# A two-layer attention and state-space kernel: the contexts' chunk sums turned and summed as a tree, and the outputs' matrices loaded behind the last row turn

## The chip, the cores and the metric

One core of one Trainium2 chip runs the whole program. The metric is the device time of one execution in microseconds. TensorE, VectorE (DVE), ScalarE (ACT), GpSimd (POOL) and SyncE (SP, which here only issues DMAs) run side by side, each through its own instructions in order; semaphores join them. ScalarE's queue issues a few DMAs too.

## What is computed

512 latent tokens and 256 context tokens of width 1024, all in fp32, go through two layers. Layer 0 mixes tokens by attention, layer 1 by a state-space model in both directions; each is followed by a gated feed-forward block with a convolution over tokens. Contexts see only contexts. In layer 1 the contexts are needed for one thing: the state at their end, `h0`, from which the latents start.

```python
def s5_scan(u, lb_re, lb_im, bb_re, bb_im, h0, reverse):      # 64 groups of 16 channels, 64 states each
    bu_re = jnp.einsum('blgc,gnc->blgn', u, bb_re)
    bu_im = jnp.einsum('blgc,gnc->blgn', u, bb_im)
    ...                                                       # h0 enters at the first token
    _, _, h_re, h_im = lax.associative_scan(_complex_combine, (a_re, a_im, bu_re, bu_im), reverse=reverse, axis=1)

for d in range(2):                                            # forward and reverse
    hc_re, hc_im = s5_scan(u_c, ..., None, reverse)           # contexts
    h0 = (hc_re[:, fin], hc_im[:, fin])
    hl_re, hl_im = s5_scan(u_l, ..., h0, reverse)             # latents
    y_l = y_l + s5_readout(hl_re, hl_im, c_re[d], c_im[d])
```

## The kernel before

Tokens are gathered in chunks of eight, so that the recurrence inside a chunk is a matrix product: 256 contexts are 32 chunks (`NCC`), 512 latents 64 (`NCL`). The matrices `Pd` (inputs of a chunk to its sum of states) and `Qd` (inputs and incoming state to the outputs) are made early in the program, stored to HBM, and loaded again tile by tile: `Pt` is the name of a loaded tile of either, `ssm_ahead` (L1378) the generator that loads them ahead of use. 32 pairs of groups make 16 contexts' tiles of 512 KB in three buffers, two pairs in each.

The contexts' part, `ssm_contexts` (L1483), runs as jobs that are written out between the matrix products `dn` of layer 0's second feed-forward product (L145 to L147, three fp32r products for one fp32 product). It loads the tokens by chunks (`xcc`, L1493), copies them into another order on ScalarE (L1405), turns them on TensorE (`pu`, L1410), and multiplies them by the `Pt` tiles (`pi`, L1435: 64 output rows, the states, by 32 columns, the chunks). ScalarE copies each result to `Bc` (L1446). `half(0)` and `half(1)` then run the recurrence over the chunks on VectorE, each for half of the groups: `ssm_spans` (L1460 to L1464) goes through eight chunks one after the other, in four spans at once, 35 operations; `ssm_carry` (L1473 to L1476) then joins the four spans in three steps. The result is `C0` (`C` in the rows). The powers of the recurrence's factors come from the table `lam`, 1 MB.

The last four steps of the feed-forward block, each of 128 tokens, are finished by the post-norm: `po<-dn` (L727), the norm's factor (L157 to L161), the sum with the stream `px` (L732, loaded at L713, stored at L1017) and the next pre-norm (L1020, L1021). The normed latents go to HBM and are read back by chunks as `xc` (L1028), the last pair of loads on ScalarE's queue. `ssm` (L1528) then copies `xc` to `xq` (L1405), turns it (L1410), multiplies it by the latents' `Pt` tiles (L1435), runs spans and carries (L1460 to L1476), makes the states (L1592 to L1603) and the outputs (`py`, L1616 and L1621) with the `Qd` tiles, of which eight buffers of 384 KB exist.

The order on each engine is set by the framework's scheduler from its own time estimates; the order of issue on SP follows from it.

Of the kernel before, what the change touches and what calls it, by code (L numbers as in the profile page):

```python
# [9 lines left out]
FT = mybir.dt.float32  # L10
# [3 lines left out]
AF = mybir.ActivationFunctionType  # L14
OP = mybir.AluOpType
# [4 lines left out]
P = 128  # L20
# [13 lines left out]
G = 64  # L34
NS = 64
GC = 16
TC = 8
NCC = CTX // TC
# [12 lines left out]
def dap(ap, off, dims):  # L51
    return bass.AP(tensor=ap.tensor, offset=ap.offset + off, ap=[list(d) for d in dims])
# [79 lines left out]
class Kernel:  # L132
# [1242 lines left out]
            self.lay_powers(lam, part, pw[:, part])  # L1375
        return lam

    def ssm_ahead(self, loads, rooms):  # L1378


        tiles = []
        rooms = [(pool, tag, bufs) for pool, tag, bufs in rooms for _ in range(bufs)]
        for i in range(len(loads)):
            while len(tiles) < min(i + len(rooms), len(loads)):
                src, gp, n = loads[len(tiles)]
                pool, tag, bufs = rooms[len(tiles) % len(rooms)]
                shape = [P, n, *src.shape[2:]]
                k = math.prod(shape[1:])
                t = pool.tile([P, 1024 if tag == "raw" else k], FT, name="Pt", tag=tag, bufs=bufs)
                t = t[:, :k].rearrange("p (a b n) -> p a b n", a=n, n=P)  # L1390
                self.nc.sync.dma_start(t, src[:, gp:gp + n])
                tiles.append(t)
            if i == 0:
                yield
            yield tiles[i]
# [24 lines left out]
    def ssm_inputs(self, mats, Bs, us, nj, both):  # L1420
# [5 lines left out]
        for gp in range(0, G // 2, R):  # L1426
# [19 lines left out]
                    nc.scalar.activation(y, x, AF.Copy)  # L1446
            yield gp

    def ssm_spans(self, pool, B, blk):

        nc, v = self.nc, self.nc.vector
        nb, ns = B.shape[1], B.shape[2] // 8
        lr, li = (x[:, 0, blk:blk + nb].rearrange("p b r d g -> p b r (d g)") for x in self.lam)
        L = B.rearrange("p b (s k) r d g -> p b s k r (d g)", k=8)
        shape = [P, nb, ns, 2, 16]
        lr, li = (x[:, :, None].to_broadcast(shape) for x in (lr, li))
        for k in range(1, 8):
            t1 = pool.tile(shape, FT, name="t1", tag="t1", bufs=1)
            t2 = pool.tile(shape, FT, name="t2", tag="t2", bufs=1)
            v.tensor_tensor(t1, L[:, :, :, k - 1], lr, op=OP.mult)  # L1460
            for b in range(nb):
                v.tensor_tensor(t2[:, b], L[:, b, :, k - 1, ::-1], li[:, b], op=OP.mult)
            v.tensor_tensor(L[:, :, :, k], L[:, :, :, k], t1, op=OP.add)
            self.mark = v.tensor_tensor(L[:, :, :, k], L[:, :, :, k], t2, op=OP.add).ins  # L1464
            yield

    def ssm_carry(self, pool, i, o, x, add):

        v = self.nc.vector
        mr, mi = (y[:, 7, 2 * i:2 * i + 2].rearrange("p b r d g -> p b r (d g)") for y in self.lam)  # L1470
        x, add, o = (y.rearrange("p b r d g -> p b r (d g)") for y in (x, add, o))
        w = pool.tile([P, 2, 2, 2, 16], FT, name="cw", tag="cw", bufs=2)
        v.tensor_tensor(w[:, 0], x, mr, op=OP.mult)  # L1473
        v.tensor_tensor(w[:, 1], x[:, :, ::-1], mi, op=OP.mult)
        v.tensor_tensor(w[:, 0], w[:, 0], add, op=OP.add)
        self.mark = v.tensor_tensor(o, w[:, 0], w[:, 1], op=OP.add).ins  # L1476
# [6 lines left out]
    def ssm_contexts(self):  # L1483

        nc, v, su = self.nc, self.nc.vector, self.su
        self.banks = (("aux", 2),)
        self.lam_tile(su.tile([P, 2048], FT, name="lam"))
        self.C0 = su.tile([P, 2, 2, 2, 2, 8], FT, name="C0")
        x = self.sb[1].tile([P, 2, 2048], FT, name="xcc", tag="B", bufs=1)
        xcc = x[:, 0].rearrange("p (s c) -> p s c", s=TC)  # L1490
        xq = x[:, 1].rearrange("p (g s c) -> p g s c", g=16, s=TC)
        for a in range(4):
            nc.sync.dma_start(xcc[NCC * a:NCC * a + NCC],  # L1493
                              dap(self.xnd, a * (D // 4), [[TC * D, NCC], [D, TC], [1, D // 4]]))
        sc = self.pool("ssmc")
        si = self.pool("ssmi")
        uc = si.tile([P, 16, 4, NCC], FT, name="uc")
        mats = self.ssm_ahead([(self.Pd, gp, 2) for gp in range(0, G // 2, 2)], ((si, "Pt", 3),))
        next(mats)
        yield  # L1500
        for _ in self.ssm_turn(xcc, xq, uc, (nc.scalar,) * 4):
            yield
        Bc = [sc.tile([P, 2, NCC, 2, 2, 8], FT, name=f"Bc{i}") for i in range(2)]

        def half(i):
            yield from self.ssm_spans(sc, Bc[i], 2 * i)
            x = Bc[i][:, :, 7]
            for s_ in range(8, NCC, 8):
                last = s_ == NCC - 8
                o = self.C0[:, i] if last else sc.tile([P, 2, 2, 2, 8], FT, name="cc", tag="cc", bufs=3)  # L1510
                self.ssm_carry(su, i, o, x, Bc[i][:, :, s_ + 7])
                x = o
                yield

        first = half(0)
        for gp in self.ssm_inputs(mats, lambda b: Bc[b // 2][:, b % 2], lambda g: uc[:, g % 16, g // 16], NCC,
                                  lambda gp: False):
            if gp >= 12:
                next(first, None)
                next(first, None)  # L1520
            yield
        for _ in first:
            yield
        yield from half(1)
        si.release()
        sc.release()

    def ssm(self):  # L1528
        tc, nc, v = self.tc, self.nc, self.nc.vector
        ps, W, su = self.ps, self.W, self.su  # L1530
        lamR, lamI = self.lam
        up = self.pool("ssmv")
        u = up.tile([P, G, NCL], FT, name="u")
        uv = u.rearrange("p (a g) j -> p g a j", a=2)
        self.banks = (("aux", 2), ("aux", 2), ("big", 3))
        xq = self.sb[1].tile([P, 4, 8, TC, GC], FT, name="xq", tag="B", bufs=1)
# [4 lines left out]
        B = [x.tile([P, 2, NCL + 1, 2, 2, 8], FT, name="B", tag="B", bufs=1) for x in (self.sb[0], up)]  # L1541
        for i in range(2):
            nc.scalar.activation(B[i][:, :, 0], self.C0[:, i], AF.Copy)
        sp = self.pool("ssms")
        st = self.pool("ssmt")
        spans = [*(self.ssm_spans(st, B[0][:, b:b + 1, 1:], b) for b in range(2)), self.ssm_spans(st, B[1][:, :, 1:], 2)]
        for gp in self.ssm_inputs(self.mats, lambda b: B[b // 2][:, b % 2, 1:], lambda g: u[:, g], NCL,
                                  lambda gp: gp < 16):
            for b in range(min((gp + 2) // 8, 2)):
# [2 lines left out]
        self.sx.release()  # L1552
        W.behind, W.fence, W.limit = (self.mark,), None, self.glu0 + 4
        W.ensure(self.glu0 + 4)
        qs = self.ssm_ahead([(self.Qd, gp, 1) for gp in range(G // 2)],
                            ((sp, "Qt", 8),))
        with tc.issue_after(self.turned_in):
            next(qs)
        sq = self.pool("ssmq")
        NL = NCL // 8  # L1560

# [8 lines left out]
        def local(i):  # L1570

            for s_ in range(NL - 1):
                o = B[i][:, :, 8 * s_ + 8]
                self.ssm_carry(su, i, o, B[i][:, :, 8 * s_], o)

        zs = [sq.tile([P, NL, 8, 32], FT, name=f"z{i}") for i in range(2)]
        for z in zs:
# [50 lines left out]
        tiles = range(LAT // P)  # L1628
# [28 lines left out]

        first(0)
        local(0)
        for blk in range(4):  # L1660
            if blk == 2:
                with tc.issue_after(self.stated):
                    first(1)
                    local(1)
            turned(blk, outputs(blk, states(blk)))
# [161 lines left out]
```

## Time and profile before

| what | value |
|---|---|
| time, median of 3 runs | 1690.97 us (1689.34 to 1693.05) |
| profiled execution | 1691.25 us, span 1689.5 us |
| TensorE, busy share of the span | 92% |
| VectorE | 63% |
| ScalarE | 41% |
| GpSimd | 4% |
| DMA, mean rate | 156 GB/s |

The time is that of a whole execution; the span runs from the first to the last record of the profile, and is 1.75 us shorter. Busy shares are means over stages that differ: an engine with 63% may be the one that everything waits for in one stretch.

### The profile page before, as it was taken

How to read it: one execution, taken by the hardware profiler on the slowest of the kernel's cores; microseconds unless marked ns; L12 is line 12 of the kernel's file. 1: busy time of each engine (PE TensorE's matmuls, PEld its weight loads, DVE VectorE, ACT ScalarE, POOL GpSimd, SP SyncE). 2: the span in 40 equal slices, each digit the busy share in tenths (PEclk: the TensorE clock that was granted, in tenths of full speed). 3: DMA queues.
4: the chain of work that ended last, by engine and by line, in shares of the span. 5: the costliest groups of instructions: out<-in, count | busy, mean ns of one | idle time of the engine just before them, and what ended most of it. 6: DMA issues, size and time to landing. Idle time of an engine off the chain costs nothing.

```text
span 1689.5 us, 25153 instructions
## 1 busy us (share of the span) xinstructions
PE 1548.3 (92%) x9652; PEld 1245.0 (74%) x9652; DVE 1071.1 (63%) x2225; ACT 695.2 (41%) x1370; POOL 67.0 (4%) x86
## 2 busy tenths in 40 slices
PE   5999689999999999989999999227999999999997
PEld 2776459888888887767788887226778887788886
DVE  4564587769777778767654847699346655455334
ACT  4465457746433433233343442331145443333322
POOL 0111140000000000000000000000011000000000
PEclk7999799999999999999999999568999999999999
DMA  9424460077345667695774685654443234433421
GB/s 301 148 71 128 166 216 26 26 247 248 132 139 174 186 172 208 134 236 143 207 257 136 195 266 200 203 197 127 151 133 117 88 112 125 127 98 114 148 75 50
DMA packets 222173, 262.96 MB, mean 156 GB/s; under 512 B 20974, under 2 KB 172438, under 8 KB 221414
## 3 DMA queue, kind: packets, MB, share of 16 engines
q1 hardware_dynamic: 221334, 260.76, 50.3%
q8 instruction: 76, 1.25, 0.3%
q10 hardware_dynamic: 336, 0.54, 0.1%
q14 instruction: 43, 0.35, 0.1%
q0 software_dynamic: 384, 0.07, 0.0%
HBM read 223.37 MB, written 35.85 MB: 153 GB/s over the span
## 4 chain that ended last, share of the span: by engine, by line
PE 80%; DVE 10%; DMA 4%; ACT 2%; SPq 2%; issue 1%; ACTq 0%; POOL 0%; DVEq 0%
PE up L145 12%; PE up L147 11%; PE up L146 11%; PE dn L145 6%; PE dn L146 6%; PE dn L147 6%; PE acc L145 2%; PE acc L147 2%; PE acc L146 2%; PE glu L147 2%; PE glu L145 2%; PE glu L146 2%; PE macc L287 2%; PE py L1621 1%; DMA wm<-in_w_mod 1%; PE wo L145 1%
## 5 line engine op out<-in xcount | busy, mean ns | idle before, releaser
L109 DVE TENSOR_TENSOR whl<-wraw,whl 128x1024 fp32r<-128x1024 f32 x206 | 250.8, 1222 | 175.5 <-ACT whl L108 173.9
L108 ACT ACTIVATE whl<-wraw 128x1024 fp32r<-128x1024 f32 x206 | 216.6, 1055 | 207.4 <-PE dn L147 100.1
L145 PE MATMUL up<-b,whl 128*128 128x256 f32 (+1 forms) x728 | 244.8, 340 | 5.8 <-ACT whl L108 4.8
L147 PE MATMUL up<-b,whl 128*128 128x256 f32 (+1 forms) x728 | 242.7, 335 | 0.0
L146 PE MATMUL up<-b,whl 128*128 128x256 f32 (+1 forms) x728 | 242.3, 335 | 0.2 <-DVE b L339 0.2
L146 PE MATMUL dn<-whl,hs 128*128 128x512 f32 x440 | 171.7, 392 | 0.0
L147 PE MATMUL dn<-whl,hs 128*128 128x512 f32 x440 | 170.9, 392 | 0.0
L145 PE MATMUL dn<-whl,hs 128*128 128x512 f32 x440 | 170.7, 392 | 0.0
L145 PEld LDWEIGHTS up<-b,whl 128*128 128x128 f32 x728 | 137.0, 189 | 32.1 <-issue 9.9
L147 PEld LDWEIGHTS up<-b,whl 128*128 128x128 f32 x728 | 137.1, 189 | 17.7 <-issue 3.4
L146 PEld LDWEIGHTS up<-b,whl 128*128 128x128 f32 x728 | 137.7, 189 | 15.9 <-issue 1.8
L862 DVE SCALAR_TENSOR_TENSOR ga<-up,cw,ga 128x511 f32<-128x511 f32 (+1 forms) x132 | 86.9, 659 | 93.3 <-ACT ga L858 91.8
L146 PE MATMUL up<-c,whl 128*128 128x512 f32 (+1 forms) x384 | 142.6, 373 | 0.1
L147 PE MATMUL up<-c,whl 128*128 128x512 f32 (+1 forms) x384 | 141.9, 372 | 0.0
L145 PE MATMUL up<-c,whl 128*128 128x512 f32 (+1 forms) x384 | 140.8, 375 | 1.0 <-DVE c L338 1.0
L858 ACT ACTIVATE ga<-up,cw 128x512 f32<-128x512 f32 x66 | 46.5, 705 | 159.9 <-PE up L147 158.3
L862 DVE SCALAR_TENSOR_TENSOR h<-up,cw,h 128x511 f32<-128x511 f32 (+1 forms) x132 | 86.8, 658 | 35.4 <-ACT h L858 34.2
L145 PEld LDWEIGHTS dn<-whl,hs 128*128 128x128 f32 x440 | 82.7, 188 | 18.4 <-ACT ga L858 0.4
L147 PEld LDWEIGHTS dn<-whl,hs 128*128 128x128 f32 x440 | 82.7, 188 | 18.0
L146 PEld LDWEIGHTS dn<-whl,hs 128*128 128x128 f32 x440 | 82.7, 188 | 17.8
L145 PEld LDWEIGHTS up<-c,whl 128*128 128x128 f32 x384 | 71.3, 188 | 18.0 <-issue 4.5
L147 PEld LDWEIGHTS up<-c,whl 128*128 128x128 f32 x384 | 72.3, 188 | 13.4 <-issue 0.4
(345 smaller groups left out, 2840.4 us busy)
## 6 DMA issues: line engine op xcount, KB each, us to landing
wraw<-in_w_up SPq DMA_DIRECT2D x88, 512.0 KB
wraw<-in_w_mod SPq DMA_DIRECT2D x80, 512.0 KB
wraw<-in_w_down SPq DMA_DIRECT2D x66, 512.0 KB
Pt<-Pd SPq DMA_DIRECT2D x32, 512.0 KB
wraw<-in_w_o SPq DMA_DIRECT2D x24, 512.0 KB
Pt<-Qd SPq DMA_DIRECT2D x32, 384.0 KB
wm<-in_w_mod SPq DMA_DIRECT2D x16, 512.0 KB
Pd<-Pb SPq DMA_DIRECT2D x16, 512.0 KB
```

The costliest lines, as they stand in the source:

```text
L108: nc.scalar.activation(w[:, 0], r, AF.Copy)
L109: e.tensor_tensor(w[:, 1], r, w[:, 0], op=OP.subtract)
L145: nc.tensor.matmul(out, a[0], b[0], start=start, stop=False)
L146: nc.tensor.matmul(out, a[0], b[1], start=False, stop=False)
L147: nc.tensor.matmul(out, a[1], b[0], start=False, stop=stop)
L287: nc.tensor.matmul(acc[32 * q:32 * q + 32], self.cT[:, k, :], w[:, 256 * q:256 * q + 256], start=(k == 0), stop=(k == KD - 1))
L858: nc.scalar.activation(o, acc, AF.Identity, scale=c[:, 1:2], bias=c[:, 3:4])
L862: nc.vector.scalar_tensor_tensor(x, acc[:, a + s:b + s], c[:, tap:tap + 1], x, op0=OP.mult, op1=OP.add)
L1621: nc.tensor.matmul(y[hs, i], x, t[hs, 2 + 2 * ri + d], start=False, stop=ri + d == 2)
```

## The change

Four edits, all in layer 1's state-space part.

1. The contexts' inputs come out by chunks. `ssm_inputs_turned` multiplies with the tokens as the stationary operand (32 columns, the chunks) and the matrix as the moving one (256 columns: two directions, real and imaginary, 64 states): 64 products of 32x256, four groups of them on the four quarters of a bank. A copy on ScalarE (`pe`, one buffer) and four turns on TensorE (`pb`) bring each result back to states by chunks, and the same copies to `Bc` follow. One group of products goes ahead of the turns of the group before.
2. The contexts' recurrence is a tree. `ssm_sums` joins neighbours, then pairs, then fours, in three levels of five operations, with powers 1, 2 and 4; `ssm_carry` takes the table as an argument.
3. The contexts use a small table `lamc` of the powers 1, 2, 4 and 8 (four loads); the full table `lam` is loaded in `ssm`.
4. The loads of the first `Qd` tiles are created ahead of the latents' inputs, and the first of those tiles is written first by a 1x1 copy on ScalarE from the last element of `xq`, so that its load comes behind the turn of `xq`.

```diff
+    def ssm_inputs_turned(self, mats, Bs, us, nj, pool):
...
+        def turn(e, gp):
+            b = self.bank([P, 2, 2, R, nj], "pb")
+            for d in range(2):
+                for ri in range(2):
+                    nc.tensor.transpose(b[:, d, ri].rearrange("p a j -> p (a j)"),
+                                        e[:, d, ri].rearrange("p a n -> p (a n)"), self.ident)
...
+            b = self.bank([P, 2, 2, 2, NS], "pi")
+            for par in range(2):
+                for i in range(R):
+                    nc.tensor.matmul(b[nj * i:nj * i + nj, par].rearrange("p d r n -> p (d r n)"), us(32 * par + gp + i),
+                                     pairs[i][:, 2 * par:2 * par + 2].rearrange("p d x -> p (d x)"),
+                                     start=True, stop=True)
+            pairs = pairs[R:]
+            e = pool.tile([P, 2, 2, 2, NS], FT, name="pe", tag="pe", bufs=1)
+            nc.scalar.activation(e.rearrange("p d r a n -> p a d r n"), b, AF.Copy)
+            if waiting:
+                turn(*waiting)
+                yield waiting[1]
+            waiting = e, gp
...
+    def ssm_sums(self, pool, B, blk, lam):
...
+        for i in range(3):
+            h, n = 1 << i, B.shape[2] >> i + 1
+            lr, li = (x[:, i, blk:blk + 2].rearrange("p b r d g -> p b r (d g)") for x in lam)
+            E, O = (B[:, :, j - 1::2 * h].rearrange("p b m r d g -> p b m r (d g)") for j in (h, 2 * h))
+            for j in range(2):
+                t = pool.tile([P, 2, B.shape[2] // 2, 2, 16], FT, name="t", tag="t", bufs=1)[:, :, :n]
+                if j:
+                    for b in range(2):
+                        v.tensor_tensor(t[:, b], E[:, b, :, ::-1], li[:, b, None].to_broadcast([P, n, 2, 16]), op=OP.mult)
+                else:
+                    v.tensor_tensor(t, E, lr[:, :, None].to_broadcast([P, 2, n, 2, 16]), op=OP.mult)
+                v.tensor_tensor(O, O, t, op=OP.add)
+                yield
...
-        self.lam_tile(su.tile([P, 2048], FT, name="lam"))
+        lam = su.tile([P, 2, 4, 4, 2, 2, 8], FT, name="lamc")
+        for i in range(4):
+            nc.sync.dma_start(lam[:, :, i].rearrange("p a b r d g -> p a (b r d g)"),
+                              dap(self.lamd, ((1 << i) - 1) * P, [[2048, P], [1024, 2], [1, P]]))
...
-            yield from self.ssm_spans(sc, Bc[i], 2 * i)
+            yield from self.ssm_sums(sc, Bc[i], 2 * i, lam)
...
+                if behind is not None and not tiles:
+                    self.nc.scalar.activation(t[0:1, 0:1], behind, AF.Copy)
...
+        qs = self.ssm_ahead([(self.Qd, gp, 1) for gp in range(G // 2)],
+                            ((sp, "Qt", 8),), xq[0:1, 3, 7, 7, 15:16])
+        next(qs)
```

The order of instructions shows where the scheduler puts the pieces. On TensorE, at the end of the feed-forward block, this stood before: the last `dn` (tokens' steps of whl_10261) are followed at once by the latents' turns, the contexts' last product being 51 `dn` further up.

```order
L146 MATMUL dn<-whl_10261,hs 128x512
L147 MATMUL dn<-whl_10261,hs 128x512
L1410 MATMUL pu<-ident,xq 128x128 x20
L1435 MATMUL pi<-u,Pt 64x64 x7
```

And this stands there now (whl_10072 is the last weight tile):

```order
L1462 MATMUL pb<-ident,pe 128x128 x4
L145 MATMUL dn<-whl_10072,hs 128x512
L146 MATMUL dn<-whl_10072,hs 128x512
L147 MATMUL dn<-whl_10072,hs 128x512 x2
L145 MATMUL dn<-whl_10072,hs 128x512
L1476 MATMUL pi<-Pt,uc 32x256 x6
L146 MATMUL dn<-whl_10072,hs 128x512
L147 MATMUL dn<-whl_10072,hs 128x512
L1476 MATMUL pi<-Pt,uc 32x256 x2
L1462 MATMUL pb<-ident,pe 128x128 x4
L1476 MATMUL pi<-Pt,uc 32x256 x6
L1462 MATMUL pb<-ident,pe 128x128 x4
L1412 MATMUL pu<-ident,xq 128x128 x24
```

The last eight products of the contexts and the last two groups of turns have moved behind the last `dn`. Further up, the products stand in pieces of 10, 6 and 2 with a group of four turns between; before they stood in five blocks of 48 and a rest of 16.

On VectorE, ahead of the post-norm's first `po<-dn` of the last two steps, the rows of half 1 now are (Bc_9514 is its tile; the carries that follow are three times the last four rows):

```order
L1503 TENSOR_TENSOR t<-Bc_9514,lamc 128x1024
L1504 TENSOR_TENSOR Bc_9514<-Bc_9514,t 128x32x32
L1501 TENSOR_TENSOR t<-Bc_9514,lamc 128x512 x2
L1504 TENSOR_TENSOR Bc_9514<-Bc_9514,t 128x32x32
L1503 TENSOR_TENSOR t<-Bc_9514,lamc 128x2x256
L1504 TENSOR_TENSOR Bc_9514<-Bc_9514,t 128x16x32
...
L1533 TENSOR_TENSOR cw<-cw,Bc_9514 128x64
L1534 TENSOR_TENSOR C_9265<-cw 128x64
L727 TENSOR_TENSOR po<-dn,rows_9253 128x512 x2
```

Before, 35 operations of `ssm_spans` stood in the same place, ahead of the same `po<-dn`; nothing else has moved past it.

On SP, behind the last `xc` loads of its queue, this is the order now, with the last waits of each row (the fourth step's pair of loads, then the outputs' and the latents' matrices):

```order
L1028 DMA xc<-po 16x8x512 [waits DMAHW1_49,DVE_49]
L1028 DMA xc<-po 16x8x512 [waits DMAHW2_49]
L1393 DMA Pt<-Qd 128x768 [waits DMAHW5_49]
L1393 DMA Pt<-Qd 128x768 [waits DMAHW6_49]
L1393 DMA Pt<-Qd 128x768 [waits DMAHW7_49,Activation_49]
L1393 DMA Pt<-Qd 128x768 [waits DMAHW0_49,DVE_49]
L1393 DMA Pt<-Qd 128x768 [waits DMAHW1_49]
```

Before, the eight `Qd` loads stood in the same place; the third of them now has a wait for ScalarE, the 1x1 copy behind the copies to `xq`, and the others stand behind it on this queue.

## Rows read from the trace of the kernel before

**Rows 1.** The table of stretches: length, busy time and instructions by engine, clock, DMA
```profile
1041.00:1056.00 15.00, 11.28 (x50) 9.01 (x48) 14.05 (x48) 1.68 (x5) 0.00 (x0) 0.99 0.05 20
1056.00:1085.00 29.00, 0.00 (x0) 0.00 (x0) 20.00 (x66) 6.88 (x16) 0.00 (x0) 0.50 0.66 205
1062.50:1063.00 0.50, 0.00 (x0) 0.00 (x0) 0.50 (x1) 0.50 (x2) 0.00 (x0) 0.50 0.53 213
1064.00:1064.50 0.50, 0.00 (x0) 0.00 (x0) 0.50 (x1) 0.00 (x0) 0.00 (x0) 0.50 0.04 8
```

**Rows 2.** TensorE's timeline, 989 to 1087 us: start, length, engine, line, operation, count, idle before
```profile
989.78 1.04 PE L1410 MATMUL pu<-ident,xcc 128*128 128x128 f32 x8
990.58 0.48 PE L145 MATMUL dn<-whl,hs 128*128 128x512 f32 x1
...
1000.43 0.39 PE L145 MATMUL dn<-whl,hs 128*128 128x512 f32 x1
1000.75 2.99 PE L1435 MATMUL pi<-uc,Pt 128*64 128x32 f32 x96
...
1004.00 0.39 PE L147 MATMUL dn<-whl,hs 128*128 128x512 f32 x1
...
1038.92 1.13 PE L1435 MATMUL pi<-uc,Pt 128*64 128x32 f32 x32
...
1051.44 0.39 PE L145 MATMUL dn<-whl,hs 128*128 128x512 f32 x1
...
1051.89 0.39 PE L147 MATMUL dn<-whl,hs 128*128 128x512 f32 x1
1086.03 4.30 PE L1410 MATMUL pu<-ident,xq 128*128 128x128 f32 x20 [33.74 <-ACT xq L1405]
```

**Rows 3.** VectorE's timeline, 1041 to 1056 us, same columns
```profile
1041.24 0.43 DVE L1460 TENSOR_TENSOR t<-Bc,lam 128x256 f32<-128x256 f32 x1 [3.10 <-ACT Bc L1446]
...
1053.18 0.23 DVE L1473 TENSOR_TENSOR cw<-Bc,lam 128x64 f32<-128x64 f32 x1
...
1055.43 0.68 DVE L727 TENSOR_TENSOR po<-dn,rows 128x512 f32<-128x512 f32 x1
```

**Rows 4.** ScalarE's timeline, 988 to 1088 us, same columns
```profile
988.24 2.19 ACT L1405 ACTIVATE xcc<-xcc 128x512 f32<-128x512 f32 x4 [3.18 <-DMA Pt<-Pd]
...
1040.09 1.12 ACT L1446 ACTIVATE Bc<-pi 128x256 f32<-128x256 f32 x2 [5.42 <-PE pi L1435]
...
1077.31 1.29 ACTq L1028 DMA_DIRECT2D xc<-po  x2
1085.34 2.19 ACT L1405 ACTIVATE xq<-xc 128x512 f32<-128x512 f32 x4 [12.07 <-DMA xc<-po]
```

**Rows 5.** TensorE's timeline at two places where the modulation stands in other work
```profile
562.88 1.07 PE L287 MATMUL macc<-wraw,cT 128*32 128x256 f32 x16
...
1383.91 0.39 PE L147 MATMUL up<-c,whl 128*128 128x512 f32 x1
1384.23 0.62 PE L287 MATMUL macc<-wraw,cT 128*32 128x256 f32 x4
...
1385.12 0.40 PE L146 MATMUL up<-c,whl 128*128 128x512 f32 x1
```

**Rows 6.** The DMA issues on SP's timeline, 1061 to 1084 us
```profile
1061.93 4.20 SPq L1017 DMA_DIRECT2D xd<-px  x2
...
1074.53 8.92 SPq L1391 DMA_DIRECT2D Pt<-Qd  x8
```

**Rows 7.** ScalarE's groups by shape, 0 to 500 us: busy, mean ns
```profile
L1213 ACT ACTIVATE tst<-ptab,sg 128x512 f32<-128x512 f32 x6 | 7.1, 1188 | 0.5 <-PE ptab L1212 0.4
```

**Rows 8.** VectorE's groups by shape, 1017 to 1060 and 1120 to 1200 us
```profile
L1462 DVE TENSOR_TENSOR t<-Bc,lam 128x128 f32<-128x128 f32 x27 | 6.7, 285 | 0.0
...
L1603 DVE TENSOR_TENSOR S<-B,z 128x1024 f32<-128x1024 f32 x4 | 4.9, 1216 | 0.0
...
L1464 DVE TENSOR_TENSOR B<-B,t 128x512 f32<-128x512 f32 x7 | 4.8, 691 | 0.2
```

More of the change, by code (lines that the diff above doesn't have):

```diff
@@ L1376, in lam_powers, with ssm_ahead @@
         return lam
-    def ssm_ahead(self, loads, rooms):
+    def ssm_ahead(self, loads, rooms, behind=None):
         tiles = []
@@ L1447, in ssm_inputs @@
             yield gp
+    def ssm_inputs_turned(self, mats, Bs, us, nj, pool):
+        nc = self.nc
+        R = P // nj
+        pairs, waiting = [], None
+        def turn(e, gp):
[4 more added lines that the diff above has]
+                                        e[:, d, ri].rearrange("p a n -> p (a n)"), self.ident)
+            o = Bs(gp // 8)
+            for d in range(2):
+                x = b[:, d, :, :, ::-1] if d else b[:, d]
+                nc.scalar.activation(o[:, :, :, d, gp % 8:gp % 8 + R].rearrange("p j r g -> p r g j"), x, AF.Copy)
+        for gp in range(0, G // 2, R):
+            while len(pairs) < R:
+                t = next(mats)
+                pairs += [t[:, i] for i in range(t.shape[1])]
+            b = self.bank([P, 2, 2, 2, NS], "pi")
[11 more added lines that the diff above has]
+            waiting = e, gp
+        turn(*waiting)
+        yield waiting[1]
@@ new lines, in ssm_sums @@
+    def ssm_sums(self, pool, B, blk, lam):
+        v = self.nc.vector
+        for i in range(3):
[11 more added lines that the diff above has]
+                yield
@@ L1465, in ssm_spans, with ssm_carry @@
             yield
-    def ssm_carry(self, pool, i, o, x, add):
+    def ssm_carry(self, pool, i, o, x, add, lam):
         v = self.nc.vector
-        mr, mi = (y[:, 7, 2 * i:2 * i + 2].rearrange("p b r d g -> p b r (d g)") for y in self.lam)
+        mr, mi = (y[:, y.shape[1] - 1, 2 * i:2 * i + 2].rearrange("p b r d g -> p b r (d g)") for y in lam)
         x, add, o = (y.rearrange("p b r d g -> p b r (d g)") for y in (x, add, o))
@@ L1486, in ssm_contexts @@
         self.banks = (("aux", 2),)
-        self.lam_tile(su.tile([P, 2048], FT, name="lam"))
+        lam = su.tile([P, 2, 4, 4, 2, 2, 8], FT, name="lamc")
+        for i in range(4):
+            nc.sync.dma_start(lam[:, :, i].rearrange("p a b r d g -> p a (b r d g)"),
+                              dap(self.lamd, ((1 << i) - 1) * P, [[2048, P], [1024, 2], [1, P]]))
+        lam = [lam[:, j] for j in range(2)]
         self.C0 = su.tile([P, 2, 2, 2, 2, 8], FT, name="C0")
@@ L1510, in half @@
                 o = self.C0[:, i] if last else sc.tile([P, 2, 2, 2, 8], FT, name="cc", tag="cc", bufs=3)
-                self.ssm_carry(su, i, o, x, Bc[i][:, :, s_ + 7])
+                self.ssm_carry(su, i, o, x, Bc[i][:, :, s_ + 7], lam)
                 x = o
@@ L1515, in ssm_contexts @@
         first = half(0)
-        for gp in self.ssm_inputs(mats, lambda b: Bc[b // 2][:, b % 2], lambda g: uc[:, g % 16, g // 16], NCC,
-                                  lambda gp: False):
+        for gp in self.ssm_inputs_turned(mats, lambda b: Bc[b // 2][:, b % 2], lambda g: uc[:, g % 16, g // 16], NCC, si):
             if gp >= 12:
@@ L1530, in ssm @@
         ps, W, su = self.ps, self.W, self.su
+        up = self.pool("ssmv")
+        self.lam_tile(up.tile([P, 2048], FT, name="lam"))
         lamR, lamI = self.lam
-        up = self.pool("ssmv")
         u = up.tile([P, G, NCL], FT, name="u")
@@ L1554, in ssm @@
         W.ensure(self.glu0 + 4)
[L1555 to L1558, printed above, removed]
         sq = self.pool("ssmq")
@@ L1573, in local @@
                 o = B[i][:, :, 8 * s_ + 8]
-                self.ssm_carry(su, i, o, B[i][:, :, 8 * s_], o)
+                self.ssm_carry(su, i, o, B[i][:, :, 8 * s_], o, self.lam)
         zs = [sq.tile([P, NL, 8, 32], FT, name=f"z{i}") for i in range(2)]
```

## The prediction, made before the changed kernel was run

> **What bounds the kernel now.** I read the page first: TensorE is by far the busiest engine, so the time moves much only where it stands still or where its stream gets longer or shorter. Then the table of stretches, which shows the one long hole of this layer [rows 1]: between 1056 and 1085 us TensorE does nothing, VectorE is busy for 20.00 of 29 us. Then TensorE's and VectorE's timelines on both sides of the hole. TensorE ends the first feed-forward block with the `dn` of 1051.89, and starts again with the turn `pu` of 1086.03, after 33.74 us idle [rows 2]. In front of the hole VectorE runs half 1 of the contexts' sums from 1041.24 on, carries from 1053.18, and only then the first post-norm step `po<-dn` at 1055.43 [rows 3]. From there a chain of VectorE and ScalarE leads to the last two `xc` loads, issued on ScalarE's queue at 1077.31, and ScalarE starts on them at 1085.34 [rows 4]. So the time of this place is made of four parts: when the last `dn` ends, plus how far half 1 sticks out behind it, plus 22 us of a chain that is not touched, plus the load of `xc`. In the kernel before, half 1 sticks out by only 55.43 − 52.12 = 3.3 us (the last `dn` is taken to end one spacing, 0.23, after its start), since nearly all of it lies beside the last 51 `dn`.
>
> **A: TensorE up to the last dn.** Removed there: 256 contexts' matmuls of 32 columns, in five blocks and a rest. One block takes 1004.00 − 1000.43 − 2 × 0.225 = 3.12 us out of the stream (the spacing of `dn` without a break is (1051.89 − 1051.44)/2 = 0.225); the rest, busy 1.13 where a block is 2.99, takes 3.12 − 1.86 = 1.26 [rows 2]. Sum 16.9 us. Added ahead of the last `dn`: by the order of the instructions one piece of 10 matmuls, six pieces of 6, five of 2, and six of four transposes. The trace has no matmul with 32 stationary columns and 256 moving ones here, but the modulation's `macc` is one in all but name [rows 5]: two instructions (four records) take 1385.12 − 1383.91 − 0.45 = 0.76 out of the stream, eight (sixteen records) are busy 1.07 against 0.62, so a second round of four costs 0.45 more. A piece of 2 is one round (0.76), a piece of 6 is two because its third and fourth column groups come twice (1.21), the piece of 10 three (1.66). Four transposes: half of the eight at 989.78, which take (990.58 − 989.78) + 0.10, so 0.45. Together 1.66 + 6 × 1.21 + 5 × 0.76 + 6 × 0.45 = 15.4. **A = −1.5 us.** Bounds: with no loss at a change of form, 14.5 rounds × 0.45 + six turns of 0.23 make 7.9, so −9; with 0.3 us of waiting at each of a dozen pieces, +2.
>
> Each `macc` piece costs about 0.3 us over its 0.45 of matmul, that is, the change of form is dear and the kernel now does twelve instead of six of them here [rows 5]. The Trainium skill, TensorEngine Tiling (Array Packing), Tiling Modes, says that a change of tiling mode drains TensorE, which speaks against cutting the inputs into small pieces between the `dn`. The same page, Overview, promises up to 4× for 32 columns; by that alone the 64 matmuls would cost 16 rounds and A would be near −9. By the rows it is −1.5.
>
> **B: TensorE at the contexts' turn.** In the order the eight first turns of `xcc` now stand 8 `dn` earlier. Before they start at 989.78, 1.5 us after ScalarE began the copies of `xcc` (988.24, after 3.18 of waiting for a DMA) [rows 2, 4]: they are on time and no more. Eight `dn` earlier is 1.8 us, which TensorE will wait. The power table ahead of `xcc` on SP's queue is 512 KB in 512-byte rows in place of 1 MB in long rows, with four issues for one. I take the landing as unchanged: **B = +1.8** (0 if the smaller table lets `xcc` land that much earlier, 3.2 if the extra issues delay it).
>
> **C: half 1 behind the last dn.** This is the large term. By the order, the last two `dn` are now followed by the rest of the inputs: two matmuls of the last group, the turn of group 6, six matmuls of the last group, its turn. Call the end of the last `dn` E. The copy `pe` of group 6 ends near E + 0.5, its turn near E + 1.3. The last six matmuls need the 16th `Pt` tile. There are three such buffers, so its load is issued only when group 6 has read tile 13, about 0.5 us ahead of E. The nearest transfer of that size with the engines free is the 512 KB store issued at 1061.93: moving by 1062.5, done by 1064.0 [rows 1, 6], 2.1 us; with what it takes to tell TensorE I take E + 3.0 (2 to 3.5). Then six matmuls to E + 4.0, the `pe` copy of 512 elements to E + 4.7 (between half of the pair of 1.12, 0.56 for 256 elements, and 1.19 for a strided copy of 512 [rows 4, 7]), turn E + 5.3, two `Bc` copies E + 6.5 (1.12 a pair).
>
> VectorE then does the whole of half 1, since its first sum reads the tile that the last copy writes. Three levels of five operations: three of 1024 and two of 512 elements, then three of 512 and two of 256, then three of 256 and two of 128. With 1.22, 0.69, 0.43 and 0.285 [rows 3, 8]: 5.04 + 2.93 + 1.86 = 9.8, and the carries, which are the same, 1055.43 − 1053.18 = 2.25. So 12.1 us, to E + 18.6. Only 2.1 less than the 14.2 of before (1041.24 to 1055.43), though operations fall from 35 to 15. `po<-dn` waits behind all of it on VectorE. Against 3.3 before: **C = +15.3** (14 to 18). The DMA engines, 5% busy from 1041 to 1056, and ScalarE cover none of it.
>
> What is queued behind: the post-norm chain with its stores, the `px` loads, which wait for half 1 in both kernels, and both pairs of `xc`. All of it shifts as one; nothing in the 22 us from `po<-dn` to the last `xc` issue depends on the removed operations.
>
> **D: the last xc load and the outputs' matrices.** Before, eight `Qd` loads of 384 KB go out on SP's queue from 1074.53 on over 8.92 us, and the last `xc` pair, issued at 1077.31, has not reached ScalarE before 1085.34, 8.0 us [rows 4, 6]. By the order, after the change two `Qd` go out there and the third waits for a 1x1 copy on ScalarE behind the `xq` copies, with five more behind it: 2.3 of 3.1 MB are out of the way. A pair that meets nothing would need about the 2.1 us of the store plus its own issue of 0.65: 2.8. With 0.8 MB and the other pair still ahead I take 4.0, so −4.0. Late next are those six `Qd` tiles, which go in front of nine `Pd` loads of the latents; seven tiles are already there, so this costs at most part of a tile, and the small copy 0.3: +0.8. **D = −3.2** (−4.7 to +0.5). The full table, loaded later, goes behind `Pd` loads far ahead of its use: nothing; if its cover is gone, 1 MB is about 3 us.
>
> **Sum:** −1.5 + 1.8 + 15.3 − 3.2 = **+12.4 us**, on the profiled 1691.25, which is 0.28 above the median of the runs: **1703.4 us** as a median.
>
> **Rivals.**
> - *The load of xc gains nothing.* Two Qd tiles and the other pair may be enough to hold it, or the six tiles then hold back the latents' `Pd`. Then D is 0 to +1: 1707. For it: the load took 8 us also because both pairs read short rows. Against it: 2.3 MB less in front. Chance 0.15. This is also the case that part of the change does not do what it says.
> - *TensorE waits inside the stream.* One `pe` buffer and two banks mean that each piece waits for ScalarE's copy of the group before, and the `Pt` tiles come in threes to groups of two. In the row order the next two matmuls stand only 4 to 12 `dn` behind, 0.9 to 2.7 us, for a copy of 0.6 to 1.2 plus ScalarE's other work. At 0.7 us for six groups A is +2.7: 1707.6. For it: no slack at the last groups. Against it: before shows no waiting for `Pt` there. Chance 0.15.
> - *The matmuls overlap fully and the dn end early.* A at −9: 1696. Against it are the `macc` rows. Chance 0.12.
> - *Not slower.* As the last, but a round costs half of `macc`'s, and so less than 5 us for all pieces: then `dn` ends 12 us earlier and the sum is within 1 us of zero, 1691 to 1692. It decides from the point where the pieces ahead of the last `dn` take under 6 us in place of 15.4; none of the rows has a round below 0.45. Chance 0.06, nearly all of it "no change".
> - *The forecast*, 1703.4, from 1699 to 1706: 0.52.
>
> **How the numbers follow.** A measurement of this kernel tells 0.2% (3.4 us) from no change. The range leaves out "not slower" and the worst pile-up of the two rivals above: 1696 to 1709. Slower by over 0.2% are all cases but "not slower" and a few mishaps: 0.90; same 0.06; faster 0.04.
>
> **What would show it.** Right: in the changed profile, about 19 us between the last `dn` and `po<-dn`, with VectorE idle for some 6 of them and the tree without a break after; some 45 us from the last `dn` to the turn `pu<-xq`, where it was 34.1; the last matmuls waiting for a `Pt` DMA; `xc` on ScalarE 4 us after its issue. Wrong for A: pieces of 2 well under 0.7 or waits named at them. Wrong for C: half 1's first operation within 4 us of the last `dn`, or operations of 1024 elements far from 1.22. Wrong for D: 7 us or more from issue to the copy. The forecast fails as a whole if VectorE runs `po<-dn` ahead of the tree, which the order excludes.

## The result: 0.7% slower, and the profile after

The changed kernel takes 1702.63 us (median of 4; 1701.72 to 1705.71), the kernel before, run beside it, 1691.20: ratio 1.0071, 95% interval 1.0053 to 1.0088, 11.4 us. The prediction said 1703.4. The profiled execution takes 1701.9 us, 10.65 more than that of before.

The two traces are laid side by side at the last `dn`. It starts at 1049.92, where it was 1051.89 [rows 2]. Those 2 us are not of the change: the `dn` that stands 205 places ahead of the last, before the contexts' first turn, is already 1.95 us earlier (984.66 against 986.61). In the profiles of e1 to e4 below, which do not differ there, it stands between 984.2 and 988.8.

TensorE's timeline of the changed kernel from the contexts' first turns, and around the last `dn` (start, length, engine, line, operation, count, idle before):

```profile
987.13 1.18 PE L1412 MATMUL pu<-ident,xcc 128*128 128x128 f32 x8 [0.95 <-ACT xcc L1407]
...
1048.59 1.06 PE L1476 MATMUL pi<-Pt,uc 128*32 128x256 f32 x12
...
1049.92 0.39 PE L147 MATMUL dn<-whl,hs 128*128 128x512 f32 x1
1050.24 0.63 PE L1476 MATMUL pi<-Pt,uc 128*32 128x256 f32 x4
1050.80 0.66 PE L1462 MATMUL pb<-ident,pe 128*128 128x128 f32 x4
1052.89 1.06 PE L1476 MATMUL pi<-Pt,uc 128*32 128x256 f32 x12 [1.44 <-DMA Pt<-Pd]
1054.71 0.66 PE L1462 MATMUL pb<-ident,pe 128*128 128x128 f32 x4 [0.76 <-ACT pe L1481]
```

The last group's matmuls stand behind the last `dn` and wait for their `Pt` tile, and the turn waits for ScalarE's copy. SP issues the load of that tile 0.9 us ahead of the end of the last `dn` (1050.15, one spacing behind its start), and the first matmul that reads it starts 3.6 us after the issue:

```profile
1049.29 0.32 SPq L1393 DMA_DIRECT2D Pt<-Pd  x1
```

VectorE's timeline in the same place, to be read against [rows 3]:

```profile
1045.13 0.22 DVE L1534 TENSOR_TENSOR C<-cw 128x64 f32<-128x64 f32 x1
1056.46 1.23 DVE L1503 TENSOR_TENSOR t<-Bc,lamc 128x1024 f32<-128x1024 f32 x1 [11.10 <-ACT Bc L1467]
1057.72 1.22 DVE L1504 TENSOR_TENSOR Bc<-Bc,t 128x1024 f32<-128x1024 f32 x1
...
1066.44 0.22 DVE L1531 TENSOR_TENSOR cw<-Bc,lamc 128x64 f32<-128x64 f32 x1
...
1068.70 0.69 DVE L727 TENSOR_TENSOR po<-dn,rows 128x512 f32<-128x512 f32 x1
```

Half 0 is done at 1045; VectorE then stands idle for 11.10 us, until the last copy to `Bc`. Half 1 takes 12.2 us, and `po<-dn` starts 18.78 us behind the last `dn`, 3.54 before. ScalarE's timeline at the load of `xc`, which answers to [rows 4]:

```profile
1090.58 1.27 ACTq L1028 DMA_DIRECT2D xc<-po  x2
1095.34 2.19 ACT L1407 ACTIVATE xq<-xc 128x512 f32<-128x512 f32 x4 [8.79 <-DMA xc<-po]
1097.43 0.19 ACT L1391 ACTIVATE Pt<-xq 1x1 f32<-1x1 f32 x1
```

From `po<-dn` to the issue of this pair 21.88 us go by, exactly as before. The pair is on ScalarE after 4.76 us, where it took 8.03.

### The profile page after: what moved, and what is told of

Read it like the earlier page. It is cut to its first block, busy times and chain, and to the rows that moved or that the text cites. A ratio compares the mean times of both kernels' runs of the same rounds, so it can differ in the third digit from the quotient of the medians.

```text
span 1700.1 us, 24423 instructions
## 1 busy us (share of the span) xinstructions
PE 1551.0 (91%) x9300; PEld 1236.9 (73%) x9300; DVE 1068.6 (63%) x2185; ACT 701.0 (41%) x1379; POOL 67.5 (4%) x86
## 4 chain that ended last, share of the span: by engine, by line
PE 76%; DVE 13%; DMA 5%; ACT 3%; SPq 2%; issue 1%; ACTq 0%; POOL 0%; DVEq 0%; POOLq 0%
PE up L145 11%; PE up L147 10%; PE up L146 10%; PE dn L147 6%; PE dn L145 6%; PE dn L146 6%; PE acc L145 2%; PE acc L147 2%; PE acc L146 2%; PE glu L145 2%; PE glu L147 2%; PE glu L146 2%; PE macc L287 1%; DMA wm<-in_w_mod 1%; PE wo L147 1%
```

## The experiments

The theory: the loss is half 1, put wholly behind the last `dn` because the turned inputs come out later; the gate on the `Qd` loads gives a part back, the tree little. The rivals are named in each expectation. Three lengths carry the comparison: from the start of the contexts' first turn to the last `dn` (T), from the last `dn` to `po<-dn` (P), and from the issue of the last `xc` pair to its first copy (X), each between the starts of two rows of the profiles.

| kernel | T | P | X | median us | ratio to before (95%) |
|---|---|---|---|---|---|
| before | 62.11 | 3.54 | 8.03 | 1691.20 | |
| changed | 62.79 | 18.78 | 4.76 | 1702.63 | 1.0071 (1.0053 to 1.0088) |
| e1_no_turning | 66.47 | 1.06 | 4.82 | 1692.05 | 0.9994 (0.9984 to 1.0005) |
| e2_gate_alone | 62.18 | 3.54 | 7.70 | 1690.05 | 0.9993 (0.9984 to 1.0003) |
| e3_tree_alone | 64.31 | 2.84 | 7.95 | 1690.59 | 0.9987 (0.9978 to 0.9997) |
| e4_no_gate | 62.77 | 18.81 | 9.58 | 1708.71 | 1.0101 (1.0084 to 1.0118) |
| e5_half1_early_data | 62.78 | 7.46 | 4.80 | 1692.37 | 1.0001 (0.9990 to 1.0013) |
| e6_tile_free_mid_group | 67.89 | 14.16 | 4.81 | 1702.39 | 1.0058 (1.0039 to 1.0077) |
| e7_gate_all_eight | 62.51 | 3.53 | 4.26 | 1688.97 | 0.9978 (0.9968 to 0.9987) |
| e8_tree_and_gate_all | 62.36 | 2.84 | 4.25 | 1688.36 | 0.9970 (0.9959 to 0.9981) |
| e9_turned_no_tree | 62.79 | 20.48 | 5.44 | 1704.69 | 1.0068 (1.0052 to 1.0084) |
| e10_turned_quarters | 62.75 | 15.15 | 5.42 | 1701.24 | 1.0047 (1.0033 to 1.0061) |
| e11_quarters_untuned_inputs | 62.39 | -0.67 | 4.25 | 1683.07 | 0.9943 (0.9930 to 0.9956) |
| e12_quarters_small_tiles | 67.98 | -0.89 | 4.27 | 1685.80 | 0.9961 (0.9948 to 0.9974) |

In the kernels with the small table ahead of `xcc` (changed, e1, e4, e5, e6, e9, e10) T starts 8 `dn`, 1.8 us, earlier in the program. The median of the kernel before, run beside each set, was 1692.36 for e1 to e4, 1692.53 for e5 to e8 and 1693.24 for e9 to e12; so the ratio compares, not the median. T, P and X come from one profiled execution of each kernel, the median from all its runs: the profiled executions of e2 and e12 were their slowest, those of e4 and e7 their fastest.

### The change's parts apart: e1 to e4

e1 goes back to the old inputs and keeps the rest; e2 and e3 put one part into the kernel before; e4 takes the gate out of the changed kernel.

```diff
 e1:
-        for gp in self.ssm_inputs_turned(mats, lambda b: Bc[b // 2][:, b % 2], lambda g: uc[:, g % 16, g // 16], NCC, si):
+        for gp in self.ssm_inputs(mats, lambda b: Bc[b // 2][:, b % 2], lambda g: uc[:, g % 16, g // 16], NCC,
+                                  lambda gp: False):
 e3, in the kernel before (ssm_sums reads the powers 1, 2, 4 from the full table):
-            yield from self.ssm_spans(sc, Bc[i], 2 * i)
+            yield from self.ssm_sums(sc, Bc[i], 2 * i, self.lam)
```

> The changed kernel, but with the contexts' inputs as before (64 rows by 32 columns, no turns, no pe copies); tree, small table and the gated Qd loads stay. Theory (the loss is half 1 behind the last dn, brought there by the turned inputs): half 1 starts some 58 dn ahead of the last one, 12.1 us before it ends, po<-dn comes within 1 us of the last dn where it was 3.5 before and 18.8 with the change; with the xc load 3.3 us shorter and 0.7 of that given back, 5 us under the kernel before, near 1686.5. Rival (the small table, the tree's operations or the gated loads cost something themselves): at or above 1691.

P is 1.06 and X 4.82, as the theory has it, and without the turned inputs the loss is gone. But nothing is won over the kernel before: T is 4.4 longer, of which 1.8 are the eight `dn`, and TensorE waited 2.0 ahead of T's start. The waits of TensorE in e1, 985 to 1060 us (engine, line, waited for: us in total, times, longest):

```profile
PE pu L1412 <- ACT xcc L1407: 2.0, 1, 2.0
PE pi L1437 <- DMA Pt<-Pd: 1.6, 3, 0.9
```

So 3.6 us are the contexts' first turn, which now stands too early, and `Pt` tiles that the old inputs ask for before they have come. Of the 1.0 more in T that no wait names, 0.8 lies in the same two blocks of matmuls that wait for the tiles: together they take 2.4 us more out of the stream than two unbroken ones, of which the profile names 1.6 as waiting. The expectation had left out both.

> The kernel before with the gated Qd loads alone. Theory: xc is on ScalarE 4.8 us after its issue in place of 8.0, 0.6 of the gain is given back behind it: 2.6 us under the kernel before, near 1688.6. Rival (the Qd loads only move into the latents' Pd loads, and what they delay there takes back the gain): no change, 1691.

Not as expected: X is 7.70. SP's and ScalarE's rows of e2 show why:

```profile
1079.72 0.80 SPq L1393 DMA_DIRECT2D Pt<-Qd  x2
```

```profile
1079.60 1.25 ACTq L1028 DMA_DIRECT2D xc<-po  x2
1087.30 2.19 ACT L1407 ACTIVATE xq<-xc 128x512 f32<-128x512 f32 x4 [11.73 <-DMA xc<-po]
1089.39 0.18 ACT L1391 ACTIVATE Pt<-xq 1x1 f32<-1x1 f32 x1
```

The gate holds the third tile and those behind it; the two ahead of it go out with the `xc` pair, and two tiles beside the pair cost it about as much as eight that start 2.8 us ahead of it (7.70 against 8.03). In e2 SP's first `Qd` load waits for the same operation on `po` as the pair. A row of SP's waits, 1070 to 1092 us, shows it:

```profile
SPq L1393 <- DVE po L1021: 2.9, 1, 2.9
```

In the changed kernel the same two are issued 2.8 us ahead of the pair (1087.76 against 1090.58), since nothing there makes them wait:

```profile
1087.76 1.08 SPq L1393 DMA_DIRECT2D Pt<-Qd  x2
```

> The kernel before with the tree alone, on the full table. Theory: half 1 takes 12.1 us in place of 14.2 and starts 4 dn (0.9 us) later by the order, so po<-dn comes about 1.2 us earlier: 1690.0. Rival (TensorE's end and ScalarE's squares hold po<-dn, not half 1): no change at all, 1691.2; or, if an operation on 1024 elements with strides costs more than 1.22, slower.

P is 0.70 shorter, and the time 0.13% lower (2.2 us, interval 0.5 to 3.7), which holds the 1.2 us expected; but T is 2.2 longer in the profile, all of it in the one block of matmuls that waits 1.7 us for `Pt` tiles, a wait that the kernel before does not have. The tree alone is worth about as little as a measurement can tell.

> The changed kernel with the Qd loads as before, free behind the xc loads. Theory: xc takes 8.0 us again from issue to copy, 2.7 us over the changed kernel, near 1705. Rival (the gate gives nothing in sum, since what waits moves on): 1702.6.

X is 9.58, 4.8 us over the changed kernel, and the ratio 0.30% higher. The gate is a gain of nearly 5 us in the changed kernel, where the theory gave it 2.7, since without it the pair takes even longer here than in the kernel before (9.58 against 8.03, with the same eight loads 2.8 us ahead); why is not shown.

### Is it half 1's wait, or the pieces in the stream: e5, e6, e9, e10

```diff
 e5:
-            yield from self.ssm_sums(sc, Bc[i], 2 * i, lam)
-            x = Bc[i][:, :, 7]
+            yield from self.ssm_sums(sc, Bc[0], 2 * i, lam)
+            x = Bc[0][:, :, 7]
...
-                self.ssm_carry(su, i, o, x, Bc[i][:, :, s_ + 7], lam)
+                self.ssm_carry(su, i, o, x, Bc[0][:, :, s_ + 7], lam)
 e6:
-            for par in range(2):
-                for i in range(R):
+            for i0 in (0, 2):
+              for par in range(2):
+                for i in (i0, i0 + 1):
```

> The changed kernel, with half 1 computed from half 0's tile in place of its own (so its values are those of other data; every instruction of TensorE and ScalarE stays, half 1 only has no last copy to wait for). Theory (the loss is half 1 waiting for pieces that come out behind the last dn): half 1 follows half 0 at once, 1045 to 1057 in the time of the changed trace, and po<-dn comes 7.4 us behind the last dn in place of 18.8: 11.4 less, near 1691. Rival (the pieces cost TensorE their time in the stream, the waits behind it only show it): 1702.6 as before.

This is the run that decides. T is the same to 0.01 us, so all the pieces are still in TensorE's stream, and the loss is gone (ratio 1.0001): VectorE's rows of e5 have half 1 directly behind half 0.

```profile
1047.68 0.23 DVE L1534 TENSOR_TENSOR C<-cw 128x64 f32<-128x64 f32 x1
1047.82 1.22 DVE L1504 TENSOR_TENSOR Bc<-Bc,t 128x1024 f32<-128x1024 f32 x1
...
1058.65 0.22 DVE L1534 TENSOR_TENSOR C<-cw 128x64 f32<-128x64 f32 x1
1058.80 0.68 DVE L727 TENSOR_TENSOR po<-dn,rows 128x512 f32<-128x512 f32 x1
```

> The changed kernel with the eight matmuls of a group in another order (both halves of pairs 0 and 1, then of 2 and 3), so that a Pt buffer comes free in the middle of a group. By the order of instructions the last matmuls then stand 13 dn ahead of the end and only the last four turns behind it. Theory: po<-dn near 14 us behind the last dn in place of 18.8, 4.8 less: 1698, with no Pt wait behind the last dn. Rival (Pt tiles come at the rate of the DMAs, not of the buffers): TensorE waits for them between the dn, the last dn is later by what the tail saves, 1702.

P is 14.16, as expected, and no `Pt` wait is left, neither behind the last `dn` nor in the stream. Yet the time did not fall: T is 5.1 longer. So neither side was right. About 2.4 of the 5.1 is work that stood behind the last `dn` in the changed kernel (two pieces and a group of turns, 0.76 + 1.21 + 0.45 by the prediction's prices). Another 1.5 is TensorE's clock in this execution. Behind the 1.9 us for which TensorE waits at the contexts' first turn, from 989 to 992 us, the granted clock (the third number from the end of the row below) is 0.50, the lower of its two levels, 1.2 in place of 2.4 GHz, and the turns and the next five `dn` are longer by that. A wait as long left the clock at 1.00 in e1, e5, e9 and e10, so nothing ties this to the edit:

```profile
989.00:992.00 3.00, 3.00 (x12) 0.50 0.78 313
```

The remaining 1.2 fits the new order of matmuls, in which a piece of four uses the same two quarters twice and takes two rounds, as a row of e6 shows (eight records, as long as the twelve of a piece of six in the changed kernel):

```profile
1052.70 1.06 PE L1477 MATMUL pi<-Pt,uc 128*32 128x256 f32 x8
```

> The changed kernel with the turned inputs but the recurrence as before, step by step (35 operations a half). Theory: half 1 stands wholly behind the last copy either way, so its full length counts: 14.2 in place of 12.1 us, po<-dn 20.9 us behind the last dn, 2.1 over the changed kernel, near 1705. Rival (the number of operations, 15 against 35, costs more than their elements, because each waits for the one before): 5 or more over it.

P is 1.70 longer, half 1 13.7 us in place of 12.2: the tree is worth 1.4 us where it stands in the open, not the 2.1 taken (the 14.2 of before had a split of `hs` in it). In the ratio, 1.0068 against 1.0071, this is below what a measurement tells.

> The changed kernel with the tree and the carries by quarters (four tiles of 8 pairs of groups in place of two of 16), so that only the last quarter waits for the last copy. Theory: behind it stand three levels of half the elements, 2.9 + 1.8 + 1.2, and the carries, 2.2 or less, 8 us in place of 12: po<-dn near 14.7 us behind the last dn in place of 18.8, 4 less, 1698.5. Rival (one of the earlier quarters is late too, since all share VectorE with the splits of the weights): 1701.

e10 makes four tiles of `Bc` and four jobs in place of two. P is 15.15, 3.6 less than in the changed kernel, near the 14.7 of the theory. The ratio is 0.24% lower, but the two intervals overlap, so P and not the time carries this. The last rows of VectorE in e10:

```profile
1059.16 0.69 DVE L1503 TENSOR_TENSOR t<-Bc,lamc 128x512 f32<-128x512 f32 x1 [2.16 <-ACT Bc L1467]
...
1064.35 0.18 DVE L1534 TENSOR_TENSOR C<-cw 128x32 f32<-128x32 f32 x1
...
1067.25 0.19 DVE L1534 TENSOR_TENSOR C<-cw 128x32 f32<-128x32 f32 x1
1067.36 0.68 DVE L727 TENSOR_TENSOR po<-dn,rows 128x512 f32<-128x512 f32 x1
```

The carries of the third quarter (its `C` is at 1064.35) stand between the operations of the last, although VectorE was idle for 2.16 us ahead of them. Each of the twelve moves its successor by 0.1 us, so an order with them ahead would give an estimated 1.2 us more; it was not run.

### A version that beats both: e7, e8, e11, e12

```diff
 e7, on the kernel before with the gate:
-                if behind is not None and not tiles:
-                    self.nc.scalar.activation(t[0:1, 0:1], behind, AF.Copy)
+                if behind is not None and len(tiles) < len(rooms):
+                    self.nc.gpsimd.tensor_copy(t[0:1, 0:1], behind)
 e11, on e8 (ssm_sums and ssm_carry take their number of blocks from the tile; the old inputs stay):
-        Bc = [sc.tile([P, 2, NCC, 2, 2, 8], FT, name=f"Bc{i}") for i in range(2)]
+        Bc = [sc.tile([P, 1, NCC, 2, 2, 8], FT, name=f"Bc{i}") for i in range(4)]
...
-        first = half(0)
+        parts = [half(i) for i in range(4)]
...
-            if gp >= 12:
-                next(first, None)
-                next(first, None)
+            for i in range((gp + 4) // 8):
+                next(parts[i], None)
+                next(parts[i], None)
 e12, on e11:
-        mats = self.ssm_ahead([(self.Pd, gp, 2) for gp in range(0, G // 2, 2)], ((si, "Pt", 3),))
+        mats = self.ssm_ahead([(self.Pd, gp, 1) for gp in range(G // 2)], ((si, "Pt", 6),))
```

> The kernel before with all eight first Qd loads held behind the xq copies (one 1x1 copy each on GpSimd), where the gate alone left two free. Theory (in the gate alone the two free tiles went out with the xc pair, at 1079.72 against 1079.60, and shared its 7.7 us): the pair now is on ScalarE 3 to 4.5 us after its issue, 3.5 less, of which the Pd loads behind give back 1: 2.5 under before, 1689. Rival (the pair's short rows set its time whatever else moves): 7.5 us as before, no change.

X is 4.26 and the ratio 0.9978, 3.7 us: this settles e2, the two free tiles were what held the pair. (Here the small copies run on GpSimd, eight in place of one on ScalarE.) ScalarE's rows of e7:

```profile
1074.19 1.27 ACTq L1028 DMA_DIRECT2D xc<-po  x2
1078.45 2.19 ACT L1407 ACTIVATE xq<-xc 128x512 f32<-128x512 f32 x4 [8.29 <-DMA xc<-po]
```

> The kernel before with the tree (on the full table) and all eight Qd loads held: the parts that gained, without the turned inputs. Theory: the gains add up, po<-dn 0.7 earlier behind the last dn, xc 3.5 shorter, at most 1.5 back from Pt and Pd waits: 3 under before, 1688. Rival: each is taken back by the Pt waits in the stream that the tree alone showed (1.7 us), no change.

0.9970, near the sum of the parts; TensorE has no `Pt` wait ahead of the last `dn` here, so that of e3 is not bound to the tree.

> The tree on the kernel before with all eight Qd loads held, and the sums by quarters. Theory: the last quarter starts 10 to 11 us ahead of the last dn and takes 8, so half 1 no longer sticks out: po<-dn 0.6 to 1.1 us behind the last dn in place of 2.84, 2 under that kernel, near 1686.5. Rival (Pt waits in the stream move the last dn): no gain over it, 1688.4.

The best kernel: 1683.07, ratio 0.9943, 0.57% or about 9.7 us under the kernel before, and clear of e8, from which it differs only in the quarters. The last quarter is done ahead of the last `dn`; VectorE's rows of e11:

```profile
1041.28 0.69 DVE L1465 TENSOR_TENSOR t<-Bc,lam 128x512 f32<-128x512 f32 x1 [1.87 <-ACT Bc L1448]
...
1049.48 0.19 DVE L1496 TENSOR_TENSOR C<-cw 128x32 f32<-128x32 f32 x1
...
1051.03 0.69 DVE L727 TENSOR_TENSOR po<-dn,rows 128x512 f32<-128x512 f32 x1 [1.36 <-ACT junk L726]
```

`po<-dn` now waits for ScalarE's square of the same `dn` tile, and runs before the last `dn` (1051.70), whose tile is not the first one that it reads. The gain over e8 is larger than expected because P could become negative (−0.67 in place of 2.84), which the expectation had not seen.

> The kernel of e11 with Pt tiles of one pair in six buffers, in place of two pairs in three, the same bytes. By the order the last contexts' matmul then stands 78 dn ahead of the end in place of 52. Theory: po<-dn already follows the last dn in e11, so an earlier end of the sums gives nothing; smaller tiles ask more issues on SP: 1686.5, same as e11. Rival (tiles come free earlier and the Pt waits in the stream go): 1 to 2 under e11. Other rival (the order asks for tiles faster than the DMAs bring them): TensorE waits 2 us or more, over e11.

T is 5.6 longer. TensorE's waits of e12, 990 to 1062 us:

```profile
PE pi L1437 <- DMA Pt<-Pd: 2.9, 2, 1.8
```

The second rival: the order asks for tiles faster than they come. The 2.9 us are half of the lengthening. Most of the other half is TensorE's clock: at the end of the longer wait and behind it, from 1022 to 1028 us, the granted clock is 0.50, the `dn` come 0.43 us apart in place of 0.227, and the next twelve cost 2.3 us more. The longer wait and that stretch of the clock:

```profile
1022.34 1.07 PE L1437 MATMUL pi<-uc,Pt 128*64 128x32 f32 x16 [1.77 <-DMA Pt<-Pd]
```

```profile
1022.00:1028.00 6.00, 5.66 (x27) 0.50 0.66 245
```

This execution is the slowest of the five, 4.1 us over their median, so T overstates the loss: the median is 2.7 us over that of e11, and the two intervals overlap a little.

## Why the prediction was right, step by step

The total is within 0.8 us of the measured one, and the mechanism is the one forecast: the turn of `xq` stands 46.0 us behind the last `dn`, where some 45 were forecast and 34.1 were before. By its terms, from the two profiled executions:

- **C, half 1 behind the last dn: +15.3 forecast, 18.78 − 3.54 = +15.24 measured.** The steps: the `Pt` tile was to be there 3.0 us behind the end of the last `dn` (1050.15), and the matmuls started at 1052.89, 2.7 behind, with the load issued 0.9 ahead of that end in place of 0.5; half 1 was to take 12.1 us and took 12.24; it was to begin 6.5 behind and began 6.3 behind. That the lateness causes the loss, and not the pieces, is shown by e5.
- **A and B, TensorE up to the last dn: +0.3 forecast, −0.02 measured** (1.95 us ahead at the 206th `dn` from the end, 1.97 at the last). The two were each too large, and their errors offset each other. T is 62.79 with 200 `dn` where it was 62.11 with 192, so the pieces take 0.68 − 8 × 0.227 = −1.1 where −1.5 was forecast. The wait at the contexts' turn was 0.95 in place of 1.8: "on time and no more" was wrong for the kernel before, in which the turn started 1.54 us after ScalarE's first copy, while in the changed kernel it starts 0.68 after it. In the other kernels with the small table this wait is 1.9 to 2.2, but for e4 (0.6); that it was short in the profiled execution is luck. The `macc` rows were a good price for the turned matmuls: a piece of six is busy 1.06, where the row had 1.07. Read as gaps between the `dn`, a piece of two takes 0.76 us out of the stream, one of six 1.19, that of ten 1.61 and four turns 0.44, together 15.2 where 15.4 was forecast.
- **D: −3.2 forecast, −2.2 measured.** The load itself fell by 8.03 − 4.76 = 3.27 (4.0 forecast). Behind it the latents' stage was taken to give back 0.8: the last `py` comes 140.57 us behind the turn of `xq`, where it was 138.81, and of these 1.8 us 1.1 are left at the last `dn` of the program. The reason for X was only half of the one given: not the six tiles held back alone, but that the two others happen to be early. That is luck: in e2, where they go out with the pair, X is 7.70. Nor does a pair that meets nothing take the 2.8 us of the prediction: it takes 4.25 to 4.27 in e7, e8, e11 and e12.
- **The rest** is the start of the program, −1.95 in these two profiles, which no step speaks of and which differs from one execution to the next, and −0.4 behind the last `dn` of the program. With these the terms make 10.7, the difference of the two profiled executions.

So the large term and its cause are right. That the total came within 0.8 us is in part luck: D missed by 1.0, A and B by 0.4 and 0.9 in opposite directions, and the runs of the changed kernel alone spread over 4 us.

The rival "TensorE waits inside the stream" did not come about in the changed kernel, whose only `Pt` wait is behind the last `dn`; in e1, e3 and e12, all with the old inputs, TensorE did wait for `Pt` tiles. "The load of xc gains nothing" is nearly what e2 shows of the same edit in the other kernel (X 7.70 in place of 8.03). That the matmuls overlap fully is refuted by T, and "not slower" by the pieces, 15.2 us where it needed less than 6. Two sums of the prediction do not come out. The bound of −9 for A counts 14.5 rounds, where its own pieces have 20 (3 + 6 × 2 + 5); these and the turns make 10.4, and A −6.5. "Not slower", with A at −12, makes about +2 by its own terms, not within 1 us of zero. Neither touches the forecast.

A further round costs 0.43 us (1.19 − 0.76), so about 0.3 us of each piece goes beyond its matmuls, and the twelve small pieces ahead of the last `dn` and their turns saved 1.1 us over the six large ones of the older form, not 9. This agrees with the weight that the prediction gave to the Trainium skill's rule that a change of tiling mode drains TensorE (TensorEngine Tiling (Array Packing), Tiling Modes). That the 0.3 us are such a drain no run here shows.

## What to carry to other kernels

Fewer and faster operations do not pay if the stage's last result comes later by more than they save (here 1.4 us against 15.2): ask of such a change where the last instruction of the producer stands in the order, against the first one that waits for its consumer, and price the whole consumer from there. If a stage must end late, cut its consumer by pieces that can start before the last one (e10, e11), since then only the last piece is in the open. When loads are held back for an urgent one, look at every load that is left beside it: two tiles issued with the pair cost it 3.4 us, the same two issued 2.8 us ahead 0.5 to 1.2.

## What the runs showed of the hardware that was not expected

- The same pair of `xc` loads (512 KB) took 4.26 us from issue to use with nothing free to go out beside it (e7), 4.76 (changed) to 5.44 (e9) with 0.8 MB issued 2.8 us ahead, 7.70 with 0.8 MB issued with it (e2), 8.03 and 9.58 with 3.1 MB from 2.8 us ahead on (before, e4). So both counted, how much the other transfer moved and when it started: 0.8 MB at the wrong time cost nearly as much as 3.1 MB. The spread between kernels with the same issues (4.76 to 5.44, 8.03 to 9.58) is not explained.
- TensorE's granted clock fell from 1.00 to 0.50 (2.4 to 1.2 GHz) in or just behind a wait of 1.88 us in e6 and of 1.77 us in e12, and came back 3 and 6 us later; behind waits of 1.9 to 2.2 us in e1, e5, e9 and e10 it stayed at 1.00. In those two executions the wait cost about twice its length in all.
- A piece of the 32 by 256 matmuls takes as many rounds as its most used quarter of the array has matmuls: two on two quarters are busy 0.63 us and six on four 1.06 in the changed kernel, but four on two quarters 1.06 as well in e6. The number of matmuls alone does not price a piece.
